# The order of 30 expert jobs in a mixture-of-experts trunk, and the batches in which their tokens are gathered

## The chip, the core and the metric

The kernel runs on one core of one Trainium2 chip. Its time is the device time of one execution in microseconds (us); of several executions the median is given. TensorE is called PE, VectorE DVE, ScalarE ACT, GpSimd POOL. SyncE (SP) issues nearly all transfers.

## The reference, cut to what matters

One layer for 256 tokens of 1024 channels in float32: a token mixer (convolution and spatial gating), then a mixture of 32 experts, of which each token takes the best 4. The second part, with what concerns the experts:

```python
logits = (xt @ w_router + b_router)
top_logits, top_idx = lax.top_k(logits, 4)          # of 32 experts
top_w = jax.nn.softmax(top_logits)
# for each expert e, for the tokens xb that chose it:
gate, up = jnp.split(xb @ w_gu[e] + b_gu[e], 2, axis=-1)   # w_gu[e]: 1024 x 2048
gate = jnp.minimum(gate, 7.0); up = jnp.clip(up, -7.0, 7.0)
act = (up + 1) * (gate * jax.nn.sigmoid(1.702 * gate))
y_e = act @ w_dn[e] + b_dn[e]                              # w_dn[e]: 1024 x 1024
# y[token] += top_w * y_e, then gate, residual and layer norm
```

An expert's weights are 12 MB: 8 MB of `w_gu` and 4 MB of `w_dn`.

## The kernel before

**Jobs.** After the mixer and the router, the kernel works through 30 jobs, one expert each, numbered 0 to 29 here. Each job has a kind that says for how many tokens it has room: C 32, B 64, A 128, W 192. The list `KINDS` names the kinds in the order of the jobs. Job 0 always takes expert 0; every other job takes the next expert of its kind's stretch in the ranking by token count (`RANK0`: W from rank 1, A from 2, B from 7, C from 14). Which experts are served, and by which kind, hangs on how often a kind stands in the list, not on the places.

**A job on PE.** The gate-up stage (`gu_mm`) has eight steps, each with one 1 MB load of `w_gu`; the down stage (`dn_mm`) has four steps, each with one 1 MB load of `w_dn` and two halves. The tokens are the stationary operand and the weights stream past. Kind A needs four full-width matmuls a gate-up step (L1164) and L1295 in the down stage. Kinds B and C hold fewer tokens and run two or four matmuls side by side in strips of the array (`cols_mm`, L1153, for the gate-up stage of both and the down stage of B; L1302 for the down stage of C). W is A and B together. Between the stages lie transposes (L1223) and the activation on DVE and ACT. The program is written job by job as gate-up of job j, then down of job j-1; the instruction order of PE is then set by a scheduler, which lets the first step of the next gate-up stage slip between the down steps. The order on DVE is as written (`manual_schedule`).

**Gathers and scatters.** `BATCHES` cuts the jobs into groups. The tokens of a batch are picked out by matmuls with one-hot matrices (`one_hots`, L939; `gather_mm`, L963, 32 matmuls a batch; `gather_out`, L970), for the next batch while the last job of the present one runs. The first batch is gathered while PE would start job 0. The result of a job, or of two B or four C together, is added to the output by a scatter (L1358, four matmuls); two small matmuls (L1119, L1120) make its weights.

**Small work.** Gathers, scatters, the activation's transposes, bias tables and the like stand in one list, `waiting`. `tick()` and `begin()` put one piece of it before and after each step, `until()` and `flush()` as many as are needed.

**Loads.** SP issues the loads in one order that never changes: `next_gu` after each gate-up step (L197), `next_dn` after each down step (L211). There are 9 buffers for `w_gu` and 4 for `w_dn`, so a load is issued when the load 9 (or 4) before it of its sort has been consumed, about 13 loads ahead of its use. After the last gate-up loads have been issued, only the 4 down buffers are left: the four down loads of job 29 wait each for a down step of job 28.

```python
N_G, N_D = 9, 4
def next_gu():                      # called after each gu_mm(job, k, raw)
    ...
        ring_g.append(load_gu(COLS[m // KC], m % KC, raw))
def next_dn():                      # called after each dn_mm(last, ci, raw)
    ...
        ring_d.append(load_dn(COLS[m // 4], m % 4, raw_x("xd", N_D)))
```

Of the kernel before, what the change touches and what calls it, by code (L numbers as in the profile page):

```python
# [28 lines left out]

KINDS = ("B", "B", "C", "C", "A", "B", "B", "C", "C", "A", "C", "C", "A", "C", "C", "A", "C", "C", "A",
         "C", "C", "W", "C", "C", "B", "B", "B", "B", "C", "C")
CAP = {"W": 192, "A": 128, "B": 64, "C": 32}
RANK0 = {"W": 1, "A": 2, "B": 7, "C": 14}
BATCHES = ((0, 1, 2, 3), (4, 5, 6), (7, 8, 9, 10, 11), (12, 13, 14), (15, 16, 17), (18, 19, 20), (21,
           22, 23), (24, 25, 26, 27), (28, 29))
NSTATIC = len(KINDS)
COLS = [j + sum(k == "W" for k in KINDS[:j]) for j in range(NSTATIC)]
NV = COLS[-1] + 1  # L40
# [36 lines left out]
def kernel(ctx, tc, a, out):  # L77
# [210 lines left out]
    seen = dict(RANK0)  # L288
    for j, kind in enumerate(KINDS):
        c0 = COLS[j]  # L290
# [633 lines left out]
    def columns(js):  # L924

        out_ = []
        for j in js:
            if KINDS[j] == "W":
                out_ += [(COLS[j], P), (COLS[j] + 1, 64)]
            else:  # L930
                out_ += [(COLS[j], CAP[KINDS[j]])]
        return out_

    def one_hots(b, eng):
        oh = tmp.tile([P, NT, 2 * P], F32R, name=nm("oh"), tag="oh", bufs=2)
        for t in range(NT):
            o = 0
            for c, n in columns(BATCHES[b]):
                eng.tensor_scalar(oh[:, t, o:o + n], iota_s[:, :n], P1[:, t, c:c + 1], None, op0=ALU.is_equal)  # L939
                o += n  # L940
        return oh
# [8 lines left out]

    jobs = [Job(k, c) for k, c in zip(KINDS, COLS)]
    for kind, size in (("B", 2), ("C", 4)):
# [23 lines left out]
    def gather(b):  # L976

        oh = ohs.pop(b)
        S = A8([P, KC, 2 * P], F32, "S")
        n = 0  # L980
        for j in BATCHES[b]:
            jobs[j].S, jobs[j].batch = S[:, :, n:n + CAP[KINDS[j]]], b
            n += CAP[KINDS[j]]
        left[b] = KC // 2

        def unit(kk):
            box = []

            def mm():
                box.append(MS())  # L990
                gather_mm(box[0], S, kk, oh, n)

            def out_():
                gather_out(S, box[0], kk, n)
                left[b] -= 1
            return [mm, out_]
        return [unit(kk) for kk in range(KC // 2)]
# [387 lines left out]

    batch_of = {j: b for b, js in enumerate(BATCHES) for j in js}
    undone = []
    for j in range(NSTATIC + 1):
# [7 lines left out]
        if job:  # L1396
            b = batch_of[j]
            if j == BATCHES[b][0] and b + 1 < len(BATCHES):
                ohs[b + 1] = one_hots(b + 1, gp)
            if j == BATCHES[b][-1] and b + 1 < len(BATCHES):  # L1400
                waiting += gather(b + 1)
# [123 lines left out]
```

## Time and profile before

| | |
|---|---|
| median of 3 runs | 1247.66 us (1247.53 to 1249.54) |
| profiled execution: its own time | 1246.66 us |
| profiled execution: span from first to last instruction | 1244.8 us |
| PE busy | 1110.8 us, 89% |
| bytes read | 446.92 MB, 360 GB/s over the span |

The mixer takes the first 300 us or so, the jobs run from 320 to 1219, then come the final layer norm and the output. A busy PE is not PE at its peak: its share says little. What the reader should watch is the rate of the transfers, slice by slice, and where it falls.

### The profile page before, as it was taken

To read this page: it belongs to the slowest core of one execution; us is meant where nothing else is said; L and a number is where in the kernel's file an instruction comes from. 1 tells how busy PE (TensorE), PEld (TensorE's weight loads), DVE (VectorE), ACT (ScalarE), POOL (GpSimd) and SP (SyncE) were. 2 spreads that over 40 slices of the span, in tenths; PEclk is the share of its full clock that TensorE was granted. 3 is DMA by queue.
4 is the path that set the end of the run, shared out by engine and by line. 5 is a ranking of instruction groups with operands and counts; after the bars stand their busy time and mean duration, and the time that the engine had idled before them with its cause. 6 is when DMAs were issued, how large, how long until landed. Compare 5 with 4: busy or idle time off the path is not lost. (4 is left out here: it accounts for less than half of the span.)

```text
span 1244.8 us, 15509 instructions
## 1 busy us (share of the span) xinstructions
PE 1110.8 (89%) x5954; PEld 576.6 (46%) x5954; DVE 478.0 (38%) x940; ACT 206.9 (17%) x348; POOL 56.1 (5%) x195
## 2 busy tenths in 40 slices
PE   1999999999998799989879999899779999999763
PEld 1997888887533343324324434334323433333221
DVE  6889999986332121211301211311202322112134
ACT  1433324533110110200100110010010101001000
POOL 6000000000200000100000010010000000000000
PEclk9999999999899899999989999999889999999796
DMA  9984336596899999999999999999999799999992
GB/s 365 378 311 160 112 117 244 174 341 255 323 390 419 419 420 419 420 419 420 419 421 418 420 419 420 419 419 420 418 419 413 299 399 406 420 420 420 420 420 100
DMA packets 68956, 449.19 MB, mean 361 GB/s; under 512 B 7377, under 2 KB 7417, under 8 KB 20704
## 3 DMA queue, kind: packets, MB, share of 16 engines
q1 hardware_dynamic: 67312, 443.84, 88.2%
q0 software_dynamic: 1552, 4.15, 0.9%
q8 instruction: 54, 0.88, 0.3%
q14 instruction: 38, 0.31, 0.1%
HBM read 446.92 MB, written 1.05 MB: 360 GB/s over the span
## 5 line engine op out<-in xcount | busy, mean ns | idle before, releaser
L1153 PE MATMUL big<-raw,S 128*32 128x512 f32 (+1 forms) x1600 | 274.1, 622 | 16.1 <-DMA raw<-in_w_gu_dram 16.1
L1330 DVE TENSOR_TENSOR ob<-big,g2c 32x256 f32<-32x256 f32 (+1 forms) x80 | 37.9, 474 | 360.9 <-PE big L1302 245.2
L1164 PE MATMUL big<-raw,S 128*128 128x512 f32 x384 | 173.4, 602 | 3.1 <-DMA raw<-in_w_gu_dram 3.1
L1153 PEld LDWEIGHTS big<-raw,S 128*32 128x32 f32 (+1 forms) x1600 | 65.5, 121 | 167.9 <-issue 119.8
L1164 PEld LDWEIGHTS big<-raw,S 128*128 128x128 f32 x384 | 71.3, 191 | 94.4 <-issue 88.6
L1302 PE MATMUL big<-raw,aT 128*32 128x256 f32 x1024 | 76.8, 440 | 26.6 <-DMA raw<-in_w_dn_dram 22.7
L525 DVE SCALAR_TENSOR_TENSOR sg<-ya,par,sg 128x256 f32<-128x256 f32 x240 | 100.0, 472 | 0.6
L1350 DVE TENSOR_TENSOR x<-x,ms 128x512 f32<-128x512 f32 x56 | 38.3, 686 | 155.8 <-PE ms L1358 155.6
L1295 PE MATMUL big<-raw,aT 128*128 128x512 f32 x192 | 86.9, 605 | 3.3 <-DMA raw<-in_w_dn_dram 3.3
L434 PE MATMUL big<-hT,raw 128*128 128x256 f32 x384 | 85.5, 379 | 0.0
L1199 ACT ACTIVATE gt<-gt 128x256 f32<-128x256 f32 (+1 forms) x46 | 21.7, 472 | 367.7 <-DVE gt L1198 356.7
L434 PEld LDWEIGHTS big<-hT,raw 128*128 128x128 f32 x384 | 71.8, 190 | 9.6 <-issue 0.5
L1302 PEld LDWEIGHTS big<-raw,aT 128*32 128x32 f32 x1024 | 32.5, 122 | 74.9 <-issue 30.5
L1153 PE MATMUL big<-raw,aT 128*64 128x512 f32 x256 | 63.0, 621 | 1.2 <-DMA raw<-in_w_dn_dram 1.2
L1358 PE MATMUL ms<-ob,ohT 128*128 128x512 f32 x112 | 58.7, 636 | 3.4 <-DVE ob L1330 2.7
L1223 PE MATMUL ms<-ident,g 128*128 128x128 f32 x224 | 39.8, 308 | 22.5 <-ACT g L1187 7.2
L1295 PEld LDWEIGHTS big<-raw,aT 128*128 128x128 f32 x192 | 36.1, 193 | 50.5 <-issue 45.9
L1223 PEld LDWEIGHTS ms<-ident,g 128*128 128x128 f32 x224 | 31.5, 207 | 58.3 <-ACT g L1187 17.9
L148 DVE TENSOR_TENSOR lo<-raw,hi 128x1024 fp32r<-128x1024 f32 x46 | 55.1, 1215 | 8.6 <-ACT hi L147 6.1
L1314 DVE TENSOR_TENSOR ob<-big,g2c 128x512 f32<-128x512 f32 x12 | 7.7, 686 | 128.2 <-PE big L1295 128.2
L436 PE MATMUL big<-hThi,hi 128*128 128x256 f32 x192 | 56.3, 294 | 0.0
L438 PE MATMUL big<-hThi,lo 128*128 128x256 f32 x192 | 55.4, 290 | 0.8 <-DVE lo L148 0.8
(327 smaller groups left out, 1231.2 us busy)
## 6 DMA issues: line engine op xcount, KB each, us to landing
raw<-in_w_gu_dram SPq DMA_DIRECT2D x240, 1024.0 KB, 19.8
raw<-in_w_dn_dram SPq DMA_DIRECT2D x120, 1024.0 KB, 19.8
raw<-in_w_mod_dram SPq DMA_DIRECT2D x24, 1024.0 KB, 7.5
raw<-in_w_in_dram SPq DMA_DIRECT2D x24, 1024.0 KB, 6.7
raw<-in_w_b_dram SPq DMA_DIRECT2D x4, 1024.0 KB, 4.9
raw<-in_w_a_dram SPq DMA_DIRECT2D x4, 1024.0 KB, 5.1
raw<-in_w_out_dram SPq DMA_DIRECT2D x4, 1024.0 KB, 8.8
x<-in_x_dram SPq DMA_DIRECT2D x1, 1024.0 KB, 8.4
```

Source lines behind the costliest of these rows:

```text
L148: ve.tensor_tensor(c.lo[q], src, f(c.hi[q]), op=ALU.subtract)
L434: pe.matmul(o, lhsT=ck.raw[:, k2 * D + n * P:k2 * D + (n + 1) * P], rhs=af[:, k], start=b0, stop=b1)
L436: pe.matmul(o, lhsT=ck.hi[k2][:, s], rhs=ahi[:, k], start=b0, stop=False)
L438: pe.matmul(o, lhsT=ck.lo[k2][:, s], rhs=ahi[:, k], start=False, stop=b1)
L525: ve.scalar_tensor_tensor(cT[:, n], ya[:, n, t:t + T], bcol(n, t), cT[:, n], op0=ALU.mult, op1=ALU.add)
L1153: pe.matmul(out_[q * n:(q + 1) * n], lhsT=S, rhs=raw[:, w0(q):w0(q) + 512], start=first_, stop=last_)
L1164: pe.matmul(job.ps[h][:, n * 512:(n + 1) * 512], lhsT=S[:, k, 0:P], rhs=raw[:, h * D + n * 512:h * D + (n + 1) * 512], start=f0, stop=f1)
L1223: pe.transpose(ps[:, i * P:(i + 1) * P], g[:, chans(c)], ident)
L1295: pe.matmul(job.pd[0][:, n * 512:(n + 1) * 512], lhsT=job.aT[:, k, 0:P], rhs=raw[:, k2 * D + n * 512:k2 * D + (n + 1) * 512], start=f0, st ...
L1302: pe.matmul(job.pd[0][q * 32:(q + 1) * 32, 0:256], lhsT=job.aT[:, k, 0:32], rhs=raw[:, k2 * D + q * 256:k2 * D + (q + 1) * 256], start=f0, ...
L1350: ve.tensor_tensor(yy, yy, box[0], op=ALU.add)
L1358: pe.matmul(box[0], lhsT=w()[r, t * P:(t + 1) * P], rhs=o(n)[r], start=i == 0, stop=i == len(parts_) - 1)
```

## The change

Only the two tables differ; no function is changed. As strings, with the places of the jobs counted from 0, the kinds are

```
before  BBCCA BBCCA CCACC ACCAC CWCCB BBBCC
after   BCCCC ABBBA CCACC BBCCA CCWCC BBACC
```

There are 8 B, 16 C, 5 A and one W in both. The batches follow the new order: the first one now holds jobs 0 to 2 (64 + 32 + 32 = 128 tokens' room) where it held jobs 0 to 3 (192), and there are nine in both.

```diff
-KINDS = ("B", "B", "C", "C", "A", "B", "B", "C", "C", "A", "C", "C", "A", "C", "C", "A", "C", "C", "A",
-         "C", "C", "W", "C", "C", "B", "B", "B", "B", "C", "C")
+KINDS = ("B", "C", "C", "C", "C", "A", "B", "B", "B", "A", "C", "C", "A", "C", "C", "B", "B", "C", "C",
+         "A", "C", "C", "W", "C", "C", "B", "B", "A", "C", "C")
...
-BATCHES = ((0, 1, 2, 3), (4, 5, 6), (7, 8, 9, 10, 11), (12, 13, 14), (15, 16, 17), (18, 19, 20), (21,
-           22, 23), (24, 25, 26, 27), (28, 29))
+BATCHES = ((0, 1, 2), (3, 4, 5, 6), (7, 8, 9), (10, 11, 12, 13, 14), (15, 16, 17, 18), (19, 20, 21),
+           (22, 23, 24), (25, 26, 27), (28, 29))
```

What this does to the instructions shows at three places. The first is DVE just ahead of the first gather, where `one_hots` writes the matrix `oh`, once for each half of the tokens (a piece of the difference, - before, + after):

```order
 L916 CAST JR<-J 32x31
-L939 TENSOR_SCALAR oh_2701<-iota_s,P_2681 128x64 x2
+L939 TENSOR_SCALAR oh_2701<-iota_s,P_2681 128x64
 L939 TENSOR_SCALAR oh_2701<-iota_s,P_2681 128x32 x2
-L939 TENSOR_SCALAR oh_2701<-iota_s,P_2681 128x64 x2
+L939 TENSOR_SCALAR oh_2701<-iota_s,P_2681 128x64
 L939 TENSOR_SCALAR oh_2701<-iota_s,P_2681 128x32 x2
```

One one-hot of a B job's 64 columns is gone from each half, so two of eight instructions. On PE the 32 gather matmuls stay and have 128 columns each where they had 192.

The second place is PE at job 1, behind the last step of job 0 (`S` holds the gathered tokens, `raw` the weights, `g` the gate-up result of job 0; a piece of the difference again):

```order
+L1153 MATMUL big_2907<-raw_2685,S_2720 32x512 x4
 L1223 MATMUL ms_2917<-ident,g_2904 128x128 x4
-L1153 MATMUL big_2907<-raw_2755,S_2722 64x512 x4
-L1153 MATMUL big_2907<-raw_2781,S_2722 64x512 x4
+L1153 MATMUL big_2907<-raw_2755,S_2720 32x512 x4
+L1153 MATMUL big_2907<-raw_2781,S_2720 32x512 x4
```

Job 1 is now of kind C: each of its eight gate-up steps runs four strips of 32 side by side where it ran two of 64. The steps stand in the same place and use the same buffers.

The third place is PE at the end, from the transposes of job 28 on: the down stage of job 27 (`aT` is its activation) and the first gate-up steps of job 29 (`S`). Before:

```order
L1223 MATMUL ms_7021<-ident,g_6987 128x128 x4
L1153 MATMUL big_6989<-raw_6869,aT_6932 64x512 x4
L1153 MATMUL big_6989<-raw_6878,aT_6932 64x512 x4
L1153 MATMUL big_7016<-raw_6840,S_6732 32x512
L1153 MATMUL big_6989<-raw_6887,aT_6932 64x512 x4
L1153 MATMUL big_7016<-raw_6840,S_6732 32x512 x3
L1153 MATMUL big_6989<-raw_6896,aT_6932 64x512 x4
L1358 MATMUL ms_7043<-ob_6900,ohT_6968 128x512
```

After the change:

```order
L1223 MATMUL ms_7021<-ident,g_6979 128x128 x4
L1295 MATMUL big_6981<-raw_6856,aT_6914 128x512 x4
L1295 MATMUL big_6981<-raw_6868,aT_6914 128x512 x4
L1295 MATMUL big_6981<-raw_6874,aT_6914 128x512 x4
L1295 MATMUL big_6981<-raw_6880,aT_6914 128x512 x4
L1153 MATMUL big_7016<-raw_6826,S_6714 32x512 x4
L1153 MATMUL big_7016<-raw_6889,S_6714 32x512 x4
L1153 MATMUL big_7016<-raw_6912,S_6714 32x512 x4
L1358 MATMUL ms_7043<-ob_7013,ohT_6992 128x512
L1153 MATMUL big_7016<-raw_6920,S_6714 32x512 x4
```

Job 27 is an A now. Its down stage has 16 full-width matmuls (L1295), and all of them stand ahead of the first gate-up step of job 29, where the 16 half-width ones of a B stood with that step among them. The same scatter of four follows. The jobs from W on are now W C C B B A C C and start with job 22; they were W C C B B B B C C from job 21.

## Rows read from the trace of the kernel before

**Rows 1.** The page, part 2: megabytes moved per second, in 40 slices of the span.

```profile
GB/s 365 378 311 160 112 117 244 174 341 255 323 390 419 419 420 419 420 419 420 419 421 418 420 419 420 419 419 420 418 419 413 299 399 406 420 420 420 420 420 100
```

**Rows 2.** The page, part 6: gate-up loads; issues, size, median time to landing.

```profile
raw<-in_w_gu_dram SPq DMA_DIRECT2D x240, 1024.0 KB, 19.8
```

**Rows 3.** Windows of 10 us: busy time (instructions) by engine, PE clock, DMA share, GB/s.

```profile
320.00:330.00 10.00, 9.78 (x37) 4.94 (x38) 2.58 (x18) 1.82 (x4) 2.70 (x6) 0.66 0.68 262
...
330.00:340.00 10.00, 10.00 (x69) 7.03 (x68) 1.60 (x9) 2.36 (x4) 0.40 (x2) 1.00 0.85 311
...
340.00:350.00 10.00, 10.00 (x46) 3.19 (x46) 3.79 (x12) 2.30 (x5) 3.87 (x10) 1.00 0.83 290
...
350.00:360.00 10.00, 10.00 (x46) 3.52 (x42) 3.89 (x11) 2.12 (x3) 0.00 (x0) 1.00 1.01 421
...
960.00:970.00 10.00, 10.00 (x31) 3.34 (x29) 0.00 (x0) 0.00 (x0) 0.00 (x0) 1.00 0.86 338
...
970.00:980.00 10.00, 10.00 (x30) 3.70 (x30) 0.00 (x0) 1.76 (x2) 0.00 (x0) 1.00 0.58 217
...
980.00:990.00 10.00, 10.00 (x114) 5.02 (x114) 4.91 (x10) 1.91 (x3) 0.00 (x0) 1.00 0.77 302
```

**Rows 4.** Timeline, TensorE, first gather: start, length, line, out<-in, records, [idle before].

```profile
320.12 0.75 PE L963 MATMUL ms<-oh,hnhi 128*128 128x192 f32 x2 [1.40 <-issue]
...
321.40 0.63 PE L963 MATMUL ms<-oh,hnlo 128*128 128x192 f32 x2
...
321.83 0.63 PE L963 MATMUL ms<-oh,hnhi 128*128 128x192 f32 x2
...
329.96 0.39 PE L963 MATMUL ms<-oh,hnlo 128*128 128x192 f32 x2
...
330.19 0.39 PE L963 MATMUL ms<-oh,hnhi 128*128 128x192 f32 x2
```

**Rows 5.** Timeline, VectorE: the eight one-hots of the first gather.

```profile
319.04 1.35 DVE L939 TENSOR_SCALAR oh<-iota_s,P 128x64 fp32r<-128x64 f32 x8
```

**Rows 6.** Timeline, TensorE: the gather of batch (28, 29), 64 columns.

```profile
1125.01 0.39 PE L963 MATMUL ms<-oh,hnhi 128*128 128x64 f32 x2
1125.23 0.39 PE L963 MATMUL ms<-oh,hnlo 128*128 128x64 f32 x2
```

**Rows 7.** Timeline, TensorE: stages of jobs of kinds A and B, transposes, a scatter.

```profile
841.38 24.30 PE L1164 MATMUL big<-raw,S 128*128 128x512 f32 x56 [1.43 <-DMA raw<-in_w_gu_dram]
...
800.64 14.00 PE L1295 MATMUL big<-raw,aT 128*128 128x512 f32 x32 [0.70 <-DMA raw<-in_w_dn_dram]
...
1073.36 12.24 PE L1153 MATMUL big<-raw,S 128*64 128x512 f32 x56
...
1086.70 1.22 PE L1223 MATMUL ms<-ident,g 128*128 128x128 f32 x8 [1.11 <-ACT g L1185]
...
1093.06 3.65 PE L1153 MATMUL big<-raw,aT 128*64 128x512 f32 x16
...
934.01 3.79 PE L1358 MATMUL ms<-ob,ohT 128*128 128x512 f32 x8
```

**Rows 8.** Timeline, TensorE: the last two jobs, both of kind C.

```profile
1191.46 2.78 PE L1153 MATMUL big<-raw,S 128*32 128x512 f32 x24
...
1199.07 0.74 PE L1223 MATMUL ms<-ident,g 128*128 128x128 f32 x4 [0.76 <-ACT g L1187]
...
1200.49 1.07 PE L1302 MATMUL big<-raw,aT 128*32 128x256 f32 x16
...
1212.71 6.53 PE L1302 MATMUL big<-raw,aT 128*32 128x256 f32 x64 [3.90 <-DVE aT L1211]
```

**Rows 9.** Line L197, 966 to 982: three loads issued 5.5 us apart.

```profile
DMA to landing us min/median/max: 4.7/4.8/5.0
```

**Rows 10.** Line L211, 1187 to 1188: the last down load of job 28.

```profile
L211 SPq DMA_DIRECT2D raw<-in_w_dn_dram x1: 333/333/333, 1187.3 to 1187.3; - x1
...
DMA to landing us min/median/max: 19.8/19.8/19.8
```

## Prediction

> **What bounds the kernel now.** I read the page's transfer rate first, because a share of busy time over 1245 us says nothing of a stage. From slice 12 (counted from 0) to 38, that is from about 373 us to the end of the jobs, it stands at 419 to 421 GB/s but for a few slices [rows 1]: the jobs wait for weights, and PE mostly waits with them. The page's part on issues says what flows: 240 gate-up loads of 1 MB, 19.8 us from issue to landing, so a long queue is always waiting [rows 2]. A job's twelve loads are 12.58 MB, at 0.42 MB/us 30.0 us (2.5 each), and 30 jobs are 900 us whatever their order. So an order can move only three things: what is lost before the stream is full, what is lost inside, and what comes after its end.
>
> The windows price the first two [rows 3]. From 320 to 350 the rates are 262, 311 and 290, against 420 a loss of 3.8 + 2.6 + 3.1 = 9.5 us: PE has started late and frees buffers slowly. From 960 to 990 they are 338, 217 and 302, a loss of 2.0 + 4.8 + 2.8 = 9.6 us: W keeps PE too long, and buffers come free one at a time. At the end the question is how the last loads follow each other; the timelines of the last jobs answer it [rows 8 to 10].
>
> **Start.** Two of eight one-hots go; the eight take 1.35 us [rows 5], so 0.34 us, straight on the path, since the gather waits for them. I take -0.3 us. The 32 gather matmuls stay. Do they get shorter with 128 columns for 192? In the first gather two take 0.43 us (321.40 to 321.83) while the granted clock is down, later 0.23 us (329.96 to 330.19) [rows 4]; the mean clock of 0.66 in 320 to 330 says that 6.8 of 10 us ran at 1.2 GHz instead of 2.4 [rows 3]. At full clock two matmuls of 64 columns take 0.22 us (1125.01 to 1125.23) [rows 6]. So between 64 and 192 columns nothing is to be gained: I take 0. The bounds are 0 and a third of the gather's 16 x 0.215 + 16 x 0.115 = 5.3 us, 1.8 us.
>
> [...]
>
> Job 1 as a C: a B's gate-up stage is 12.24 us for 56 of 64 records, 14.0 us in all [rows 7]; a C's is 2.78 us for three steps, 0.87 a step and 7.0 in all [rows 8]. PE gains 7 us there, but the stream is full by then (421 from 350 to 360 [rows 3]), and freeing buffers earlier only lengthens the queue. Cost and gain 0, from both sides: a lower clock in four C in a row would also be hidden, as a C takes 12.5 us of PE in 30.
>
> **Middle.** PE's work for a job, from rows 7 and 8: A 27.5 (gate-up) + 13.8 (down) + 2.4 (16 transposes) + 3.8 + 0.8 (scatter and its weights) = 48.3 us; B 14.0 + 7.2 + 1.2 + 2.3 (half a scatter) = 24.7; C 7.0 + 3.7 + 0.7 + 1.1 = 12.5; a gather 3.7. Against 30.0 us of loads A puts PE 18.3 us behind, B takes 5.3 off, C 17.5. The new stretch A B B B A goes: 18.3, then 13.0, 7.7, 2.4, plus two gathers 9.8, with the second A 28.1, and two C clear it. How much may PE be behind before transfers are lost? W is worth A + B, 73.0 + 3.7 - 30.0 = 46.7 us, from level, and lost 9.6 [rows 3]: so about 37 us. 28.1 fits: cost 0, upper bound below (rival 3). W itself keeps its neighbours, A C C ahead and C C B behind, so its loss stays, 30.0 us later.
>
> **End.** Here I expect the change to be felt. With 13 buffers a load is called for long ahead, but the last four down loads (job 29) have only the four down buffers: each is issued when a down step of job 28 ends. Before, that down stage starts at 1200.49 and each step takes 1.07 us [rows 8]; the last load of job 28 lands at 1187.3 + 19.8 = 1207.1 [rows 10], and four more at 2.5 end at 1217.1. A load that finds no queue takes 4.8 us to land [rows 9]. For a seamless stream the first of job 29 must land at 1209.6, be issued by 1204.8, and the down stage of job 28 must start by 1203.7. Before there are 3.2 us to spare.
>
> After, job 27 is an A, and only four jobs stand between it and W. PE's position: before, the gate-up stage of job 25 (second B after W C C) ends at 1073.36 + 12.24 = 1085.6 [rows 7]. After, job 26 stands in that place, one job later: 1115.6. From there, in the order that the rows of the change give:
> - transposes with the wait for ACT 1.1 + 1.2, down stage of B 7.2, gate-up of A 27.5, gather of 64 columns 32 x 0.11 = 3.6: 1156.2;
> - down stage of B 7.2, A's transposes 1.1 + 2.4, scatter 3.8, weights twice 0.8, gate-up of C 7.0: 1179.3;
> - transposes 1.4, down stage of A 13.8, gate-up of C 7.0, scatter 3.8: 1205.3;
> - wait 0.8 and transposes with weights 1.4 (1199.07 to 1200.49): 1207.5.
>
> The loads for all this land earlier, so nothing in it waits for a transfer: before, PE sat idle for them here. So job 28's down stage starts at 1207.5, 3.8 us past 1203.7. The first down load of job 29 is issued at 1208.6, lands at 1213.4, the last at 1220.9: 3.8 us later than before. DVE's work between the two down stages (PE waits 3.90 us for `aT` [rows 8]) then ends near 1215 and is hidden behind the landings. Bounds: 0, if PE makes up 3.8 of 92 us; 8, if waits on DVE and ACT that I left out add 4.
>
> The Trainium skill, "DMA: Bandwidth & Descriptors", section "Anatomy of one DMA — SWDGE (gpsimd) path", fits a lone transfer as 2.0 us + bytes / 436 GB/s, for 1 MB an estimate of 4.4 us. The trace's 4.8 is on another path and decides; by the page the end would come 0.4 us earlier.
>
> **Sum.** +3.8 - 0.3 = +3.5 us. The profiled execution took 1246.66 us (span 1244.8 and 1.9 around it) and would take 1250.2; it lies 1.0 below the median of the runs, which would be 1247.66 + 3.5 = 1251.2 us.
>
> **Rivals.**
> 1. *The end stays hidden.* The time is that of the stream, and PE reaches job 28's down stage by 1203.7. For it: PE has slack over the whole, a scheduler may put small work where my chain counts it in full. Against: PE is without a pause in the chain, and each term is a measured row. Time 1247.66 - 0.3 = 1247.4, not slower.
> 2. *The start pays.* The gather does shrink by a third (1.8 us), and with the shorter idle ahead of it PE's clock does not drop: 6.8 us at half speed less, 3.4 us. Place: 318 to 328 us; all of it counts, since 9.5 us are lost there. It decides if the granted clock in 320 to 330 is near 1. For it: the idle ahead shrinks. Against: of the one-hots' 1.35 us three quarters stay, and PE waits for them as before. With the end as forecast 1247.66 + 3.8 - 5.5 = 1246.0; with the end hidden 1242.2.
> 3. *The middle starves.* A B B B A goes past 37 us. Its margin is 9 us; a half clock like that of rows 3 (3.4 us) twice and DVE waits would use it up. Time: some 4 us lost on top, 1255.
>
> **How the numbers follow.** What a measurement of this kernel can tell from no change is 0.2%, 2.5 us: 1245.2 to 1250.2. Forecast 0.60, rival 1 0.22, rival 2 0.10, rival 3 0.08. The forecast's own range is 1249 to 1254; I put 0.13 of its 0.60 under 1250.2. Slower: 0.47 + 0.08 = 0.55. Faster: the part of rival 2 with a hidden end and some unknown, 0.08. Same: 0.13 + 0.22 + 0.02 = 0.37. The range, 1246.0 to 1255.0, takes in rival 1 and the milder form of rival 2 and leaves out what lies past rival 3.
>
> **What would show it.** In the profile after: rate 421 without a dip between 420 and 960; the same dip of some 9.6 us beginning 30 us later, near 990; PE without waits for transfers from about 1115 to 1207; job 28's down stage starting near 1207 with all its loads landed; a hole of about 4 us in the rate just after; the last landing near 1221, and everything behind it 3 to 4 us later. A granted clock of 0.66 in 320 to 330 again speaks against rival 2. I am wrong if job 28's down stage starts before 1204, if the early stretch loses clearly less than 9 us, or if a dip shows under the jobs 5 to 10.

## The result

The change makes the kernel slower: 1256.42 us (median of 7 runs, 1254.37 to 1257.52) where the kernel before took 1247.66 in the same session (7 runs, 1245.12 to 1253.01). The ratio is 1.0065 with a 95% interval of [1.0046, 1.0085], so +8.1 us [5.7, 10.6]; the bare medians differ by 8.8. The forecast was 1251.2 with a range of 1246.0 to 1255.0: the sign is right, the time lies above the range.

The profiled execution of the changed kernel has a span of 1254.7 us (before 1244.8) and a time of 1256.42. Part 2 of its page, megabytes moved per second in 40 slices of the span, answers to [rows 1]:

```profile
GB/s 364 375 310 165 101 135 235 184 333 266 310 407 418 420 419 418 421 418 420 388 406 419 420 419 419 419 419 418 419 420 420 391 309 390 419 420 419 420 335 108
```

Two things are new. Slices 19 and 20 (596 to 659 us) fall to 388 and 406 where there was 419 or more, and the slice before the last falls to 335 from 420. The windows of the changed kernel price them and the two losses that were there before (columns as in [rows 3]):

```profile
320.00:330.00 10.00, 9.91 (x39) 5.23 (x40) 2.41 (x17) 1.61 (x4) 3.40 (x8) 0.66 0.71 268
330.00:340.00 10.00, 10.00 (x67) 6.99 (x66) 1.67 (x10) 2.50 (x5) 0.40 (x2) 1.00 0.85 327
340.00:350.00 10.00, 10.00 (x48) 3.14 (x48) 3.94 (x12) 1.94 (x4) 2.84 (x6) 1.00 0.74 279
...
600.00:610.00 10.00, 10.00 (x36) 5.45 (x35) 0.00 (x0) 3.06 (x6) 0.00 (x0) 1.00 1.01 410
610.00:620.00 10.00, 10.00 (x49) 3.83 (x47) 0.49 (x1) 3.36 (x5) 2.92 (x8) 1.00 0.90 354
620.00:630.00 10.00, 8.80 (x48) 3.61 (x44) 6.61 (x12) 1.26 (x2) 0.00 (x0) 1.00 0.97 395
630.00:640.00 10.00, 9.29 (x55) 3.34 (x55) 3.50 (x6) 0.97 (x2) 0.00 (x0) 1.00 0.98 378
990.00:1000.00 10.00, 10.00 (x31) 3.46 (x30) 0.00 (x0) 0.00 (x0) 0.00 (x0) 1.00 0.92 377
1000.00:1010.00 10.00, 10.00 (x31) 3.37 (x30) 0.00 (x0) 0.00 (x0) 0.00 (x0) 1.00 0.58 216
1010.00:1020.00 10.00, 10.00 (x90) 4.21 (x90) 0.94 (x3) 3.04 (x3) 0.00 (x0) 1.00 0.63 228
...
1200.00:1210.00 10.00, 10.00 (x68) 2.64 (x64) 5.32 (x11) 0.42 (x1) 0.00 (x0) 1.00 0.95 395
1210.00:1220.00 10.00, 6.08 (x83) 3.04 (x75) 2.95 (x8) 1.16 (x3) 0.00 (x0) 1.00 0.46 175
```

Counted against 420, the start loses 3.6 + 2.2 + 3.4 = 9.2 us (before 9.5). The stretch from 600 to 640 loses 0.2 + 1.6 + 0.6 + 1.0 = 3.4 us; before it ran at 418 to 420. The dip of W, the job of 192 tokens, stands 30 us later and takes 1.0 + 4.9 + 4.6 = 10.5 us (before 9.6). The rest of the loss is at the end, where TensorE (PE) and the last loads show it better than a rate does. First the timeline of PE, which answers to [rows 8]; jobs 27, 28 and 29 are A, C and C here:

```profile
1185.66 13.90 PE L1295 MATMUL big<-raw,aT 128*128 128x512 f32 x32
1199.49 2.78 PE L1153 MATMUL big<-raw,S 128*32 128x512 f32 x24
...
1211.76 0.74 PE L1223 MATMUL ms<-ident,g 128*128 128x128 f32 x4 [0.76 <-ACT g L1187]
...
1213.18 3.66 PE L1302 MATMUL big<-raw,aT 128*32 128x256 f32 x64
1220.73 2.82 PE L1302 MATMUL big<-raw,aT 128*32 128x256 f32 x32 [3.89 <-DVE aT L1211]
1224.68 1.93 PE L1302 MATMUL big<-raw,aT 128*32 128x256 f32 x16 [1.12 <-DMA raw<-in_w_dn_dram]
1227.19 1.67 PE L1302 MATMUL big<-raw,aT 128*32 128x256 f32 x16 [0.58 <-DMA raw<-in_w_dn_dram]
```

Job 28's down stage begins at 1213.18 and runs its 64 records in one piece without a wait for a load. Before, each of its steps but the first waited for one:

```profile
1202.23 1.07 PE L1302 MATMUL big<-raw,aT 128*32 128x256 f32 x16 [0.67 <-DMA raw<-in_w_dn_dram]
1204.73 1.81 PE L1302 MATMUL big<-raw,aT 128*32 128x256 f32 x16 [1.42 <-DMA raw<-in_w_dn_dram]
1207.22 1.59 PE L1302 MATMUL big<-raw,aT 128*32 128x256 f32 x16 [0.68 <-DMA raw<-in_w_dn_dram]
```

As the steps of this stage end, from 1214.3 to 1216.9, the last four loads are called for. The first and the last of them in the line of down loads (issue time, then time to landing), which answer to [rows 10]:

```profile
L211 SPq DMA_DIRECT2D raw<-in_w_dn_dram x1: 333/333/333, 1214.3 to 1214.3; - x1
...
DMA to landing us min/median/max: 4.7/4.7/4.7
...
L211 SPq DMA_DIRECT2D raw<-in_w_dn_dram x1: 332/332/332, 1216.9 to 1216.9; - x1
...
DMA to landing us min/median/max: 10.2/10.2/10.2
```

They land from 1214.3 + 4.7 = 1219.0 to 1227.1. The last load of job 28 lands at 1211.6 (read from the same trace; before 1207.1). So 7.4 us lie between two landings that a full queue puts 2.5 apart, 4.9 lost, and 0.6 more is lost among the four: 5.5 us. Middle and end make 8.9 us, against 8.1 measured over all runs and 9.9 between the spans of the two profiled executions. Runs of the kernel before lie up to 8 us apart, so a single trace shows where time goes and not to the last microsecond how much.

### The profile page after: what moved, and what is told of

It is laid out like the page before. It is cut to its first block, busy times and chain, and to the rows that moved or that the text cites. A ratio compares the mean times of both kernels' runs of the same rounds, so it can differ in the third digit from the quotient of the medians.

```text
span 1254.7 us, 15503 instructions
## 1 busy us (share of the span) xinstructions
PE 1113.5 (89%) x5954; PEld 573.1 (46%) x5954; DVE 478.3 (38%) x938; ACT 207.2 (17%) x348; POOL 58.3 (5%) x197
## 5 line engine op out<-in xcount | busy, mean ns | idle before, releaser
L1153 PE MATMUL big<-raw,S 128*32 128x512 f32 (+1 forms) x1600 | 281.5, 634 | 29.4 <-DMA raw<-in_w_gu_dram 29.4
L1302 PE MATMUL big<-raw,aT 128*32 128x256 f32 x1024 | 73.6, 418 | 24.7 <-DMA raw<-in_w_dn_dram 20.7
L1295 PE MATMUL big<-raw,aT 128*128 128x512 f32 x192 | 85.1, 595 | 0.4 <-DMA raw<-in_w_dn_dram 0.4
L1302 PEld LDWEIGHTS big<-raw,aT 128*32 128x32 f32 x1024 | 30.9, 116 | 72.0 <-issue 27.5
L148 DVE TENSOR_TENSOR lo<-raw,hi 128x1024 fp32r<-128x1024 f32 x46 | 55.4, 1221 | 11.5 <-ACT hi L147 7.5
L1295 PEld LDWEIGHTS big<-raw,aT 128*128 128x128 f32 x192 | 35.9, 190 | 45.5 <-issue 44.6
L437 PE MATMUL big<-hTlo,hi 128*128 128x256 f32 x192 | 56.2, 293 | 0.1
```

The source lines that it names most:

```text
L148: ve.tensor_tensor(c.lo[q], src, f(c.hi[q]), op=ALU.subtract)
L437: pe.matmul(o, lhsT=ck.hi[k2][:, s], rhs=alo[:, k], start=False, stop=False)
L1153: pe.matmul(out_[q * n:(q + 1) * n], lhsT=S, rhs=raw[:, w0(q):w0(q) + 512], start=first_, stop=last_)
L1295: pe.matmul(job.pd[0][:, n * 512:(n + 1) * 512], lhsT=job.aT[:, k, 0:P], rhs=raw[:, k2 * D + n * 512:k2 * D + (n + 1) * 512], start=f0, st ...
L1302: pe.matmul(job.pd[0][q * 32:(q + 1) * 32, 0:256], lhsT=job.aT[:, k, 0:32], rhs=raw[:, k2 * D + q * 256:k2 * D + (q + 1) * 256], start=f0, ...
```

## Experiments

Eleven kernels ran, in three groups. In a group all share the runs of the kernel before, and each ratio is to those; a ratio of 1.001 is 1.25 us. Before's median was 1247.56 us in the first group (28 runs), 1249.23 in the second (27) and 1248.29 in the third (17). The theory: the loss has two places that add, 3.4 us in the middle, because PE's arrears come up to what the buffers hold, and 5.5 at the end, because job 29's down loads wait for a late job 28. The rivals: only one place counts, the start takes part, or W does.

### Half the change

**First half.** Jobs 0 to 14 in the order of the change, the others as before.

```diff
-KINDS: BBCCABBCCACCACC ACCACCWCCBBBBCC
+KINDS: BCCCCABBBACCACC ACCACCWCCBBBBCC
```

> Jobs 0 to 14 and their batches as in the change, jobs 15 to 29 as before. Theory (two places: the stretch A B B B A starves the transfers by 3 to 4 us, the A at job 27 delays the last down loads by 5 to 6 us, the start is worth nothing): before + 3.4 us, a dip in the transfer rate between 600 and 640 of about 3 us, no hole at the end. Rival 1 (all of the loss is at the end): equal to before within 1 us, no dip. Rival 2 (the loss at 600 to 680 is chance, as such runs differ by 2 us): no dip in this profile.

Measured: 1250.4 us, ratio 1.0020 [1.0004, 1.0037], +2.5 us [0.5, 4.6]. The time alone would leave room for rival 1; the dip below does not. **Second half.** The reverse:

```diff
-KINDS: BBCCABBCCACCACC ACCACCWCCBBBBCC
+KINDS: BBCCABBCCACCACC BBCCACCWCCBBACC
```

> Jobs 0 to 14 as before, jobs 15 to 29 and their batches as in the change. Theory: before + 5.5 us, no dip at 600 to 640, a hole of about 5 us in the rate just after job 28's down loads, job 28's down stage starting 6 to 9 us later than before's 1200.5. Rival 1 (all of the loss is at the end): before + 8.8 us.

Measured: 1253.55 us, ratio 1.0043 [1.0031, 1.0054], +5.4 us. Job 28's down stage starts at 1209.3, 8.8 us later than before, as expected. The two add up to 7.9, the change itself is 8.1. Two windows of each, the first half's ahead:

```profile
610.00:620.00 10.00, 10.00 (x46) 4.81 (x46) 0.48 (x1) 4.39 (x7) 3.17 (x10) 1.00 0.83 314
...
1200.00:1210.00 10.00, 7.12 (x47) 2.55 (x43) 0.00 (x0) 0.97 (x2) 0.00 (x0) 0.70 1.01 417
```

```profile
610.00:620.00 10.00, 7.91 (x52) 3.46 (x51) 1.17 (x2) 0.97 (x2) 0.00 (x0) 1.00 1.01 419
...
1200.00:1210.00 10.00, 9.24 (x65) 3.25 (x65) 2.20 (x4) 0.97 (x2) 0.00 (x0) 1.00 0.50 206
```

Each half has its own dip (314 in the middle, 206 at the end) and not the other's. There are two places, and they add. Over all traces of this document, the four of kernels with the early stretch A B B B A (the change, this first half, the change with early down loads and the change with two lists) lose 3.1 to 4.3 us between 590 and 690, the nine others 0.2 to 0.3. The middle's loss is no chance.

### The start alone

Jobs 1 and 3 of the order before exchanged, the first batch of three jobs, so that the start is that of the change and the rest is not. The batches are ten here, one gather more than in either kernel.

```diff
-KINDS: BBCCA BBCCA ...    BATCHES: (0,1,2,3), (4,5,6), ...
+KINDS: BCCBA BBCCA ...    BATCHES: (0,1,2), (3,4), (5,6,7,8), ...
```

> Jobs 1 and 3 of the order before are exchanged (B C C B A for B B C C A) and the first batch holds three jobs, so the first gather has 128 columns and job 1 is a C, as in the change; from job 4 on the kinds are those of before. Theory (start 0, the loss comes from the middle and the end): no difference, +0 us within 1. Rival (the start of the change pays or costs): -3 or +3 us.

Measured: 1248.42 us, ratio 0.9993 [0.9981, 1.0005], -0.9 us. The interval holds zero and leaves out 3 us either way. The smaller first gather and a C as job 1 are worth nothing that can be measured.

### The middle mended, the end mended, and both

**Middle.** In the change jobs 4 and 8 are exchanged, so A B B B A becomes A B B C A: one job of 32 tokens, which pays PE's arrears back faster than a B, stands ahead of the second A. The first two batches change with it, to jobs 0 to 3 and 4 to 6.

```diff
-KINDS: BCCCCABBBACC...
+KINDS: BCCCBABBCACC...
```

> The change with jobs 4 and 8 swapped in kind, so that A B B B A becomes A B B C A (first batch then 160 columns). Theory: no dip between 560 and 660, 3.4 us under the change, before + 5.5 us. Rival 2 (that loss was chance): like the change, before + 8.8 us.

Measured: 1253.42 us, ratio 1.0041 [1.0024, 1.0057], +5.1 us [3.0, 7.1]. Against the change's 8.1 [5.7, 10.6] the time alone is no proof, but the window that fell to 354 in the change is full again:

```profile
610.00:620.00 10.00, 9.37 (x66) 4.20 (x63) 7.15 (x14) 1.64 (x3) 0.40 (x2) 1.00 1.01 419
```

**End.** The change, with job 29's four down loads issued into gate-up buffers, which are free by then, so that they wait for gate-up steps and not for the down steps of job 28.

```diff
     def next_gu():
...
+        elif m < NSTATIC * KC + 4:
+            raw = ...            # the gate-up buffers go on in turn
+            ring_e.append(load_dn(COLS[NSTATIC - 1], m - NSTATIC * KC, raw))
     def next_dn():
...
-        if m < NSTATIC * 4:
+        if m < NSTATIC * 4 - 4:
```

> The change, with the four down loads of job 29 put into gate-up buffers that have no more gate-up loads to take, so that they no longer wait for down steps of job 28. Theory (the end is late because these loads wait for four buffers): the hole after 1210 goes, job 29's down stage runs without waiting for loads, about 4.2 us in place of 8.2; 4.0 us under the change, before + 4.8 us. Rival (the end is late because PE itself comes late there, whatever the buffers): like the change, before + 8.8 us, job 29's down stage starting as late and ending as late.

Measured: 1252.11 us, ratio 1.0038 [1.0023, 1.0054], +4.7 us. The end of its transfers, and PE's last down stage:

```profile
1200.00:1210.00 10.00, 9.24 (x53) 2.43 (x50) 3.46 (x6) 0.72 (x2) 0.00 (x0) 1.00 1.01 418
1210.00:1220.00 10.00, 6.11 (x91) 3.49 (x95) 3.85 (x10) 0.80 (x2) 0.00 (x0) 0.99 0.96 394
```

```profile
1211.26 3.66 PE L1306 MATMUL big<-raw,aT 128*32 128x256 f32 x64
1218.82 5.35 PE L1306 MATMUL big<-raw,aT 128*32 128x256 f32 x64 [3.89 <-DVE aT L1215]
```

(L1306 is L1302, four lines further down in this kernel.) The hole is gone: 394 where the change had 175, and job 29's down stage no longer waits for loads: the last of the four landed at 1219.1, 0.3 us after the stage had begun. The other traces agree: the change, its second half alone, the change with its middle mended and the change with two lists have a window of 175 to 206 GB/s between 1200 and 1220, the two kernels with early down loads in the order of the change none under 394. The stage took 5.35 us and not the expected 4.2; the granted clock, 0.99 in the window shown, was 0.84 in the next. What is left of the lateness is PE's own chain, two down stages with VectorE's 3.89 us between them. The time, +4.7 us [2.9, 6.7], again lies under the change's by less than the two intervals can tell apart. **Both amendments:**

> The change with both amendments: jobs 4 and 8 exchanged (A B B C A for A B B B A) and the four down loads of job 29 issued into free gate-up buffers. Theory of two places that add: the middle's 3 us and 4.8 of the end's 5.5 us are back, so before + 0.7 to + 1.5 us. Rival (the two share a cause, or a third place exists): before + 3 us or more.

Measured: 1250.04 us, ratio 1.0008 [0.9996, 1.0020], +1.0 us. The interval in microseconds is [-0.5, 2.5], clear of the change's [5.7, 10.6]: nearly the whole loss is undone by the two, and what remains cannot be told from zero. A third place is not needed.

**The same loads early in the order before:**

> The order before with job 29's four down loads issued into free gate-up buffers. Theory (before the change the last four down loads are called for in time, with some 3 us to spare, so the wait for a down step of job 28 costs nothing there): no difference, within 1 us. Rival (that wait costs in either order, and its removal is a gain of its own): before - 4 to - 5 us, as it was between the change and the change with early down loads.

Measured: 1250.7 us, ratio 1.0014 [1.0001, 1.0027], +1.7 us [0.1, 3.4]. It is no gain, so the wait for a down step of job 28 costs something only where job 28 is late. Why it came out at +1.7 and not within 1 is open: in its trace the stream ahead of the end is some 4 us later, which no edited line explains. Some 3 us of this lie in W's dip and behind it (the three windows from 960 to 990 ran at 286, 166 and 279 GB/s), which lose about 15 us here and 12 to 14 in every other trace.

### How far PE may be behind

Jobs 5 and 9 of the order before exchanged: two full jobs side by side.

```diff
-KINDS: BBCCABBCCACCACC...
+KINDS: BBCCAABCCBCCACC...
```

> The order before with jobs 5 and 9 exchanged, so that two jobs of 128 tokens stand side by side early on (B B C C A A B C C B C C A C C); the second half as before. By the walk PE is then 36.6 us behind, and 40 with a gather. Theory (room of 9 + 4 buffers x 2.5 us less a lone landing of 4.8, 27.7 us): some 8 us are lost (6 to 12) around 480 to 560 us, before + 8. Rival (the prediction's room of 37 us): 0 to 3 us.

Measured: 1256.27 us, ratio 1.0064 [1.0044, 1.0084], +8.0 us. Two of its windows:

```profile
500.00:510.00 10.00, 10.00 (x41) 3.89 (x40) 4.12 (x7) 0.63 (x1) 0.00 (x0) 1.00 0.85 312
...
530.00:540.00 10.00, 10.00 (x30) 3.92 (x28) 0.83 (x2) 0.00 (x0) 0.00 (x0) 1.00 0.80 296
```

From 490 to 550 its six windows lose 9.8 us. With a room of 37 us an order that puts PE 36.6 to 40 behind would have lost 0 to 3, so that room is refuted. The smaller one fits, as an estimate of where losses begin. It does not give their size: arrears past 27.7 by 0.4 us (the change's middle), 9 to 12 (this run) and 19 (W) went with losses of 3.4, 8.0 and 12.3 us.

### Work taken away from beside job 0 and W

The trace had also offered a way to gain: both of the losses of 9 us are times in which PE hands buffers back late, and in both PE does small work between its steps. So the small work was put into two lists, `waiting` and `slack`; `slack` is used when `waiting` is empty, and rests beside the gate-up stages of job 0 and W.

```diff
-    def begin():
-        if waiting and not active:
-            u_ = waiting.pop(0)
+    def begin(free=False):
+        if (waiting or slack and (free or not resting[0])) and not active:
+            u_ = (waiting or slack).pop(0)
...
+        resting[0] = j == 0 or (job is not None and job.kind == "W")
...
-            waiting += [tail_unit(), bias_unit(0), bias_unit(1), weight_unit(), gate_unit()] + start_units()
+        if j == 1:
+            waiting[:0] = ... bias_unit(0), bias_unit(1) ...
+            waiting += [gate_unit(), weight_unit()]
+            slack += [tail_unit()] + start_units()
...
-            waiting += scatter_units(undone)
+            slack += scatter_units(undone)
```

**With the order before:**

> The order before, with small work in two lists: tail, weight, start and scatter units go into a second list that rests beside job 0's gate-up stage and beside W's, and the two bias units stand in job 1's steps. About 6 us of PE work leave job 0's stage and about 4 leave W's. Theory (PE, late in handing back buffers, makes both losses of 9 us): each loss shrinks by 2 to 5 us, before - 4 to - 8 us, 1241.5. Rival (job 0's loss is set by the half clock and the lone landings, W's by W itself): -1 to +1 us.

Measured: 1242.05 us, ratio 0.9936 [0.9916, 0.9955], -8.0 us. Windows of the start and of W:

```profile
320.00:330.00 10.00, 9.77 (x39) 5.76 (x40) 0.49 (x5) 1.82 (x4) 2.75 (x6) 0.66 0.67 255
330.00:340.00 10.00, 10.00 (x51) 3.92 (x52) 0.00 (x0) 1.82 (x4) 3.84 (x10) 1.00 1.00 378
340.00:350.00 10.00, 10.00 (x62) 5.65 (x60) 0.83 (x2) 0.43 (x1) 0.00 (x0) 1.00 1.02 424
```

The start loses 3.9 + 1.0 = 4.9 us where it lost 9.5. This is no chance: from 320 to 360 the ten traces without two lists lose 9.0 to 10.9 us, the three with them 4.6 to 4.9. W's dip did not shrink (3.7 + 6.1 = 9.8 us; its windows ran at 264 and 163 GB/s): the 3.8 us of scatter still stood in W's first gate-up step, because it had left the list one job earlier. That half of the expectation failed. The time lies at the far end of the theory's range, but the windows show 4.6 us at the start and no other gain. The spans of the two profiled executions, 1241.8 and 1244.8, differ by only 3.0 us: the one of before lies 2.6 us below its group's median and this one 1.6 above. What made the rest of the 8.0 us [5.6, 10.5], no trace shows.

**With the list resting in the job ahead of W too:**

```diff
-        resting[0] = j == 0 or (job is not None and job.kind == "W")
+        resting[0] = j == 0 or "W" in KINDS[j:j + 2]
```

> The order before with two lists as in the run before, and the second list now rests in the job ahead of W too, so that the scatter of job 18 (3.8 us of PE) leaves W's first gate-up step and comes behind W's gate-up stage. Theory (PE is busy without a pause from W's start to about 1063 us, so what is put off is paid inside the same stretch): the dip at 960 to 990 shrinks by 2 to 4 us, those from 1010 to 1060 grow by as much, and the time is that of two lists without it, before - 4 to - 8 us. Rival (W's dip is a loss of its own): 3 to 4 us better than that, before - 9 us or less.

Measured: 1239.32 us, ratio 0.9926 [0.9908, 0.9945], -9.2 us [-11.5, -6.9]. This is the fastest of all. The two windows of W's dip:

```profile
960.00:970.00 10.00, 10.00 (x31) 3.41 (x30) 0.00 (x0) 0.00 (x0) 0.00 (x0) 1.00 0.60 234
970.00:980.00 10.00, 10.00 (x95) 4.58 (x93) 1.80 (x5) 3.04 (x3) 0.00 (x0) 1.00 0.70 265
```

They lose 4.4 + 3.7 = 8.1 us, 1.7 less than without the rest. The dip begins earlier here, though: with the window from 950 to 960 (384 GB/s, in the run before 404) it takes 9.0 us for 10.2, 1.2 less. The dip behind W (1010 to 1060) loses 2.8 where it lost 3.1. So these two traces don't show the time put off paid back in the same stretch, as the theory had it, nor the rival's 3 to 4 us. One trace of each cannot settle it, since the change's order with early down loads and the order with the start alone changed, with nothing moved beside W, lose about 12 us in W's dip and behind it, as much as this kernel. The intervals of the two kernels overlap; how much this second step is worth stays open.

**With the order of the change:**

> The order of the change, with the same two lists. Theory (start and W give back 4 to 8 us as with the order before; the middle's 3 us and the end's 5.5 us stay, because four jobs behind W do not work off what is put off): before + 1 to + 4 us, 1250. Rival (with the lists the four jobs of 32 tokens take up the work and the order pays): below before's order with two lists, so -6 us or less.

Measured: 1254.14 us, ratio 1.0036 [1.0021, 1.0051], +4.5 us, half a microsecond above the theory's range. The lists give back about 3.6 us against the change without them (8.1 less 4.5, from two groups of runs), at the start (387 and 421 GB/s in the windows from 330 to 350); the hole at the end stays (182 from 1200 to 1210). The order of the change doesn't pay with two lists either: with them the order before is 12 us faster.

## Why the prediction was half right

**Start: right, but for 0.3 us.** Two one-hots went, PE's wait ahead of the first gather fell from 1.40 to 1.06 us, and the matmuls of 128 columns took as long as those of 192: two in 0.43 us at half clock, then in 0.22, as this timeline of the changed kernel shows beside [rows 4]:

```profile
319.96 0.69 PE L963 MATMUL ms<-oh,hnhi 128*128 128x128 f32 x2 [1.06 <-issue]
...
320.86 0.63 PE L963 MATMUL ms<-oh,hnhi 128*128 128x128 f32 x2
321.29 0.63 PE L963 MATMUL ms<-oh,hnlo 128*128 128x128 f32 x2
...
329.93 0.39 PE L963 MATMUL ms<-oh,hnhi 128*128 128x128 f32 x2
330.15 0.39 PE L963 MATMUL ms<-oh,hnlo 128*128 128x128 f32 x2
```

The granted clock was 0.66 again, so rival 2 had nothing to stand on, and the start alone measured zero. Even the forecast's 0.3 us was not kept: the landing that ends the stream's slow stretch came at 350.6 us where it came at 350.9, but by 355.9 the landings of the two traces coincide.

**Middle: wrong, and this is the step that failed.** The forecast put it at 0, and 3.4 us were lost, at the jobs 5 to 10 for which the prediction had named a dip as a sign that it is wrong. The walk of arrears was good: it put PE 28.1 us behind with the second A. In the trace of the changed kernel the last gate-up load of that job was issued at 569.9 and landed 14.5 us later, at 584.4, and PE's step on it is this one (pieces of a gather stand between the last steps of the stage):

```profile
608.57 3.60 PE L1164 MATMUL big<-raw,S 128*128 128x512 f32 x8
```

It ends at 612.2, 27.8 us after the landing. The two figures are near each other, but not the same measure: the walk also counts the A's down stage, which comes later, and the trace counts from a landing. What failed was the room, "about 37 us", taken as W's 46.7 us of arrears less the 9.6 it lost. That subtraction has two faults. It left out what was lost behind W in the kernel before, 2.7 us more:

```profile
1020.00:1030.00 10.00, 10.00 (x62) 3.90 (x65) 5.30 (x11) 1.25 (x4) 0.00 (x0) 1.00 0.90 339
...
1050.00:1060.00 10.00, 10.00 (x66) 3.62 (x60) 3.44 (x9) 0.42 (x1) 0.00 (x0) 1.00 1.00 389
```

And it took the loss for the whole excess over the room: two full jobs side by side were 9 to 12 us past the room that follows here, and lost 8.0. The room should have been counted from the buffers, with two numbers that stood in the prediction: 13 loads of 2.5 us are 32.5, and a load that finds no queue takes 4.8 to land, so the stream is whole only while a load is called for at least 4.8 us before its turn: 27.7 us. The walk's 28.1 then says that the middle is at its edge, though not that 3.4 us are lost there. The down loads show that the queue ran dry: between 617 and 623 three of them are issued and land in 5.1 to 6.4 us, little more than the 4.8 of a load that finds no queue.

```profile
L211 SPq DMA_DIRECT2D raw<-in_w_dn_dram x3: 332/332/333, 617.6 to 622.9; - x3
...
DMA to landing us min/median/max: 5.1/6.2/6.4
```

Rival 3 had the place right and about the price (4 us, 1255), with a chance of 0.08 that the wrong room had set. Its way there, PE past 37 us by a half clock and waits, is not what happened: the granted clock was 1.00 from 460 to 640, and less lateness sufficed.

**W: right.** The same dip stands 30 us later; with what is lost behind it, it comes to 12.6 us, before to 12.3, a difference that one trace of each can't tell from none.

**End: the mechanism right, the term too small.** The forecast had job 28's down stage start at 1207.5 and lose 3.8 us. It started at 1213.2, 5.7 us later, and 5.5 were lost, within the bounds given, 0 to 8. The chain was to begin with the end of job 26's gate-up stage at 1115.6; in PE's timeline of the changed kernel it ends at 1106.45 + 12.24 = 1118.7. From there to 1213.2 are 94.5 us where the terms added up to 91.9, 2.6 short; which of them were short is not worked out here. The stream itself reaches the end 4.5 us later than before (1211.6 for 1207.1), of which the middle's 3.4 are the larger part, so against the stream the start is only 1.2 us later than forecast. The last landings add 0.6 us that I had not counted. That the last landing sets the end, and not DVE's work between the two down stages, was right as well: PE waits 3.89 us for `aT`, until 1.7 us after the first of the four loads has landed, and then still for the third and the fourth.

**Sum.** Forecast: -0.3 + 0 + 0 + 3.8 = +3.5 us. Shown: about 0 + 3.4 + 0 + 5.5 = 8.9 by the windows and landings, 2.5 + 5.4 = 7.9 by the halves, 8.1 by the change itself.

## What to carry to other kernels

How far the compute engine may fall behind a stream of loads can be estimated from the buffers: their number times the time of a transfer, less the time a transfer takes when nothing is queued ahead of it. That says about where losses begin, not how large they are. Do not read it off a place that already loses time. Where the last loads have fewer buffers than the others, walk the engine's work back from there to the last point at which it had arrears; and where the stream waits for an engine to hand back a buffer, look first at the small work that stands between its steps, since moving it gained 8.0 us here, and no order of the jobs that ran gained anything clear of noise.

## What was not expected of the hardware

A gather matmul of 64, 128, 192 or 256 columns takes nearly the same time when each has new weights: 0.11 us at full clock for the first three and 0.12 for the last (in the changed kernel a pair of 256 columns follows the next after 0.24 us). And single landings in a full queue come 1 to 1.5 us late, in either kernel and at other places: before at 814.1 us (1.0), after at 668.5 and 877.1 (1.5 each), though those loads had been issued 13 to 21 us before. The rate does not fall around them (401 to 430 GB/s in windows of 2 us); the cause, and whether they cost time, no run here shows.
